# A two-layer mLSTM and retention trunk: when the heads' attention begins, and how layer 1's norm is transposed

## The chip, the cores and the metric

The kernel runs on one core of one Trainium2 chip. A core has five engines, each with a queue of its own: TensorE (PE in the profile, with PEld for its weight loads), VectorE (DVE), ScalarE (ACT), GpSimd (POOL) and SyncE (SP), which here issues the DMAs. SBUF is the memory on chip, PSUM the memory that PE writes its products to, DRAM lies outside. The metric is the time on the device in microseconds (us); lower is better.

## The reference

The input x has 1024 rows of 1024 columns. There are two layers, each with four mLSTM heads and four retention heads, 256 columns to a head:

```
for l in range(2):
    shift, scale, gate = split(silu(c) @ w_ada[l] + b_ada[l], 3)
    h = rmsnorm(x, norm_g[l]) * (1 + scale) + shift
    mq, mk, mv, mo, mz, mi, mf, rq, rk, rv, rz = split_cols(h @ w_in[l])
    mq, mk = silu(causal_conv4([mq, mk]))                 # along the rows, 4 taps
    y_m = sigmoid(mo) * layernorm(mlstm(mq, mk, mv, mi, mf)) * silu(mz)
    y_r = layernorm(retention(rotary(rq), rotary(rk), rv)) * silu(rz)
    x = x + gate * (concat(y_m, y_r) @ w_out[l])
return rmsnorm(x, final_g)
```

For mlstm and retention, row t of a head's output is a sum over the rows s up to t of (q_t . k_s) v_s with a weight that decays with t - s: in retention by a constant of the head, in mLSTM by gates computed from mi and mf, with a running maximum and a division at the end. All is float32.

## The kernel before

A float32 product is made of three matmuls on operands split in a high and a low part (`mm3`: lines 145, 146, 147); a split is a rounded copy on ACT (line 614) and a subtraction (line 615) on POOL or DVE. The projections' products go to PSUM tiles `pp`, four of them, those of attention and the transposes to `pa`, also four. The 1024 rows are two halves of 512 rows, and four chunks of 256 rows (`j` = 0 to 3). `hT[k][half]` is the normed input, transposed, for block k of 128 columns.

**Order.** PE's order is the order of the program text (`manual_schedule` for PE); the order of the other queues is set by a scheduler from the dependencies and its own estimates. The main loop runs units of projection work; after each comes a `tick`, which lets every launched generator take one step (`yield n` waits n ticks). A unit is 12 matmuls of 512 columns, or 24 of 256 in the values' projection `v_path`, which has eight units; after every second one a chunk's values are split (`v_split`, lines 600, 601, 604: two ACT copies, two DVE subtractions and, for mLSTM, two small casts). `launch(gen, d)` starts a generator d ticks later.

**A head.** Each head (`hg` = 0 to 7; 0 to 3 mLSTM, 4 to 7 retention) runs its gate projections (`gate_path`), its q and k projections (`qk_ml`, `qk_ret`), its values' projection and the generator `attention`. The steps of `attention` are: for mLSTM the load and the making of the decay masks `dm` of chunks 0 and 1 (`dm_load`, `dm_make`: lines 748, 750, 756, 757), then `scores(0)` and `scores(1)`, then for each chunk `values(j)`, `update` (the running state, split into `cH`, `cL`), `scores(j + 2)` and `finish(j)`. `scores` multiplies q by k on PE (line 765 in its diagonal form), multiplies the product by the mask on DVE (779, 780, 782, 789, 790), splits the result into `sH` (ACT) and `sL` (POOL) and loads the mask of chunk j + 2 into the buffer of its own (two buffers). `values(j)` multiplies `sH`, `sL` by the split values. The rows of k that `update` needs come back from DRAM (`k_rows`, lines 665, 666).

For heads 1 and 2 attention is launched 7 ticks, for head 3 4 ticks behind the start of `v_path`. For heads 4 to 7 it is launched when both projections are done; head 4 runs `v_path` ahead of q and k, the others behind. Between `scores(1)` and `values(0)` there is one tick, for head 0 two. Behind head 1 of layer 0 the rotary tables are made (`rotary_tables`, lines 374 to 390) in steps of their own. Retention's rotary tables are loaded again at the end of head 3 (`load_rotary`).

**The output projection** runs in two halves of the rows, each with two column halves (`out_units`, lines 952 to 956 for its loads of `g` and `ndr`). When layer 0's rows of a half are done, `norm_later` scales them and, in eight steps, transposes four blocks on PE (line 315), scales and shifts the result from PSUM (lines 321, 323) and splits it to layer 1's `hT[k][half]`. For half 0 this runs beside the output projection of half 1.

## Time and profile before

| | us |
|---|---|
| median of 3 runs | 2312.35 (2310.91 to 2312.63) |
| the profiled execution, its own time | 2311.88 |
| its span, first to last instruction | 2310.0 |

| engine | busy us | share of the span |
|---|---|---|
| PE | 2277.8 | 99% |
| DVE | 1353.2 | 59% |
| ACT | 907.1 | 39% |
| POOL | 823.5 | 36% |

How the rows are read. A timeline row has start, duration, engine, line, operation, output<-inputs and shape; matmuls are pipelined, so a row of PE lasts longer than the distance to the next one's start, and it is that distance that adds up. A row of the waits has the engine and line that waited, what it waited for, and the total, the number and the longest in us. A row of the groups has the shape, xcount, busy us and mean ns, and behind the last bar the engine's idle time ahead of it with what ended it. A row of the windows has the stretch, its length, busy us (x instructions) of PE, PEld, DVE, ACT and POOL, the granted TensorE clock (1.00 is full), the DMA engines' busy share and GB/s.

### The profile page before, as it was taken

What the parts mean: (1) busy time and instruction counts of PE and PEld (TensorE: products, weight loads), DVE (VectorE), ACT (ScalarE), POOL (GpSimd) and SP (SyncE); (2) the same over time, 40 slices, a digit from 0 to 9 for tenths busy, and PEclk for the clock granted to TensorE, in tenths of its full rate; (3) what the DMA queues carried; (4) which work ended last, traced back from release to release, by engine and by line L of the source; (5) the groups of instructions that cost most, each with busy time, mean ns of one, the idle gap of its engine ahead of it and who ended that gap; (6) DMA issues with size and microseconds to landing.
All of it is one profiled execution on the core that took longest, in us unless ns stands there. A gap on an engine that the chain in (4) does not pass through costs nothing.

```text
span 2310.0 us, 34281 instructions
## 1 busy us (share of the span) xinstructions
PE 2277.8 (99%) x12447; PEld 1958.2 (85%) x12447; DVE 1353.2 (59%) x2835; ACT 907.1 (39%) x1768; POOL 823.5 (36%) x817
## 2 busy tenths in 40 slices
PE   7999999999999999999999999999999999999998
PEld 5888888889988888888888889888898888988886
DVE  7477688556555555584536665555563545556753
ACT  5535433444332323353434544344443323224442
POOL 1343424333343334222552434233334334341323
PEclk9999999999999999999999999999999999999999
DMA  8223232324433533486532322322323333436762
GB/s 257 80 64 98 73 84 80 82 74 116 120 109 88 150 83 87 128 258 217 177 92 57 84 72 77 84 74 69 81 70 89 81 87 93 124 81 205 240 231 78
DMA packets 328761, 259.44 MB, mean 112 GB/s; under 512 B 79732, under 2 KB 263804, under 8 KB 328592
## 3 DMA queue, kind: packets, MB, share of 16 engines
q1 hardware_dynamic: 328592, 257.27, 38.6%
q8 instruction: 97, 1.59, 0.3%
q14 instruction: 72, 0.59, 0.1%
HBM read 201.58 MB, written 55.61 MB: 111 GB/s over the span
## 4 chain that ended last, share of the span: by engine, by line
PE 91%; DVE 3%; DMA 3%; issue 1%; POOL 1%; ACT 1%; SPq 0%; POOLq 0%; DVEq 0%; ACTq 0%
PE pp L145 24%; PE pp L146 24%; PE pp L147 24%; PE pa L146 5%; PE pa L147 5%; PE pa L145 5%; PE pa L765 2%; DMA b<-in_w_ada_dram 1%; DMA b<-in_x_dram 1%; PE pa L315 0%; DMA raw<-in_w_ada_dram 0%; POOL wL L615 0%; POOL sL L615 0%; DVE b L266 0%; DMA b<-in_w_in_dram 0%
## 5 line engine op out<-in xcount | busy, mean ns | idle before, releaser
L145 PE MATMUL pp<-b,wH 128*128 128x512 f32 x1776 | 703.7, 396 | 1.1 <-ACT b L1137 1.1
L146 PE MATMUL pp<-b,wH 128*128 128x512 f32 x1776 | 700.2, 394 | 0.3 <-DVE b L1140 0.2
L147 PE MATMUL pp<-b,wL 128*128 128x512 f32 x1776 | 700.2, 394 | 0.0
L615 POOL TENSOR_TENSOR wL<-raw,wH 128x512 fp32r<-128x512 f32 x338 | 450.1, 1338 | 507.4 <-ACT wH L614 466.8
L147 PEld LDWEIGHTS pp<-b,wL 128*128 128x128 f32 x1776 | 333.9, 188 | 79.0
L146 PEld LDWEIGHTS pp<-b,wH 128*128 128x128 f32 x1776 | 334.2, 188 | 72.2 <-DVE b L1140 2.0
L145 PEld LDWEIGHTS pp<-b,wH 128*128 128x128 f32 x1776 | 334.4, 188 | 71.5 <-ACT b L1137 1.6
L614 ACT CAST wH<-raw 128x512 fp32r<-128x512 f32 x402 | 246.1, 616 | 322.8 <-PE pp L147 93.8
L145 PE MATMUL pp<-wH,b 128*128 128x256 f32 (+1 forms) x1152 | 353.0, 306 | 0.7 <-DVE g L543 0.7
L147 PE MATMUL pp<-wH,b 128*128 128x256 f32 (+1 forms) x1152 | 352.8, 306 | 0.0
L146 PE MATMUL pp<-wL,b 128*128 128x256 f32 (+1 forms) x1152 | 352.2, 306 | 0.0
L615 POOL TENSOR_TENSOR b<-acc,b 128x256 fp32r<-128x256 f32 (+1 forms) x208 | 200.8, 984 | 322.8 <-ACT b L614 315.2
L145 PEld LDWEIGHTS pp<-wH,b 128*128 128x128 f32 x1152 | 216.9, 188 | 12.3 <-DVE g L543 1.6
L147 PEld LDWEIGHTS pp<-wH,b 128*128 128x128 f32 x1152 | 216.6, 188 | 11.4
L146 PEld LDWEIGHTS pp<-wL,b 128*128 128x128 f32 x1152 | 216.7, 188 | 10.8
L632 DVE SCALAR_TENSOR_TENSOR acc<-pp,cols,acc 128x511 f32<-128x511 f32 (+2 forms) x192 | 142.5, 742 | 43.2 <-ACT acc L627 41.2
L614 ACT CAST b<-acc 128x256 fp32r<-128x256 f32 (+1 forms) x208 | 93.7, 487 | 187.4 <-DVE acc L709 127.6
L615 POOL TENSOR_TENSOR sL<-th,sH 128x384 fp32r<-128x384 f32 (+1 forms) x64 | 61.0, 953 | 236.5 <-ACT sH L614 171.9
L145 PE MATMUL pa<-wH,b 128*128 128x512 f32 x256 | 101.1, 395 | 0.0
L147 PE MATMUL pa<-wH,b 128*128 128x512 f32 x256 | 101.0, 394 | 0.0
L146 PE MATMUL pa<-wL,b 128*128 128x512 f32 x256 | 100.9, 394 | 0.0
L636 ACT ACTIVATE th<-acc 128x512 f32<-128x512 f32 x64 | 40.5, 632 | 146.3 <-DVE acc L634 79.3
(255 smaller groups left out, 3439.3 us busy)
## 6 DMA issues: line engine op xcount, KB each, us to landing
raw<-in_w_in_dram SPq DMA_DIRECT2D x274, 256.0 KB
raw<-in_w_out_dram SPq DMA_DIRECT2D x128, 256.0 KB
gdr<-g SPq DMA_DIRECT2D x64, 256.0 KB
ndr<-zt SPq DMA_DIRECT2D x128, 128.0 KB
raw<-in_w_ada_dram SPq DMA_DIRECT2D x64, 256.0 KB
g<-gdr SPq DMA_DIRECT2D x64, 256.0 KB
acc<-ndr SPq DMA_DIRECT2D x64, 256.0 KB
acc<-kdr SPq DMA_DIRECT2D x192, 64.0 KB
```

Source lines behind the costliest of these rows:

```text
L145: PE.matmul(o, lt[0], rt[0], start=start, stop=False)
L146: PE.matmul(o, lt[0], rt[1], start=False, stop=False)
L147: PE.matmul(o, lt[1], rt[0], start=False, stop=stop)
L614: A.copy(dst[0], src)
L615: eng.tensor_tensor(dst[1], src, f(dst[0]), ALU.subtract)
L632: V.scalar_tensor_tensor(acc[:, d:], pt[:, 0:HALF - d], wcol, acc[:, d:], ALU.mult, ALU.add)
L636: A.activation(th, acc, AF.Tanh, scale=0.5)
L765: PE.matmul(pd, kk[i][:, o:o + P], qd, start=dt == 0 and i == 0, stop=dt == 1 and i == 1)
```

## The change

Heads 1 to 7 launch `attention` with no delay ahead of `v_path`, so that its first step is taken at the first tick of the values' projection. Between `scores(1)` and `values(0)` there is still one tick for heads 1 to 3; for the retention heads there are now two. Head 4 runs q and k first and its values' projection behind, as the others do, and head 5's first gate projection takes the place that head 4's values' projection had. In `norm_later` the first half isn't transposed by PE: DVE transposes blocks of 32 x 32 (`V.transpose`), four DMAs for each quarter of the columns store them to DRAM (`hdr`) so that the blocks fall in place, two loads bring the transposed tiles back into the buffers of `dm`, and DVE scales and shifts them from SBUF. The second half stays as it was.

```diff
--- before.py
+++ after.py
@@ -912,7 +912,7 @@
         scores(0)
         yield 1
         scores(1)
-        yield 2 if hg == 0 else 1
+        yield 1 if 0 < hg < 4 else 2
         for j in range(NCH):
             whole = j in WHOLE
             values(j, (0, 1) if whole else (0,))
@@ -1013,12 +1013,42 @@
         G.tensor_tensor(rs[:, 0:n], s, mhalf[:, 0:n], ALU.pow)
         return [rs[:, tt:tt + 1] for tt in range(n)]
 
+    hdr = [dpool.tile([8, 32, HALF], F32, name=f"hdr{s}") for s in range(4)]
+
     def norm_later(l, xt, ss, hT, half):
         sst = row_rstd(ss, "nrm")
         norm_scale(xt, sst)
-        yield 4
-        for k in range(KT):
-            norm_split(l, norm_transpose(xt, k), hT, half, k)
+        if half:
+            yield 4
+            for k in range(KT):
+                norm_split(l, norm_transpose(xt, k), hT, half, k)
+                yield 1
+            return
+        yield 1
+        for s in range(4):
+            z = wt("zt", 1024, 1)
+            z4 = z.rearrange("p (b t c) -> p t b c", b=8, c=32)
+            for tt in range(4):
+                V.transpose(z4[:, tt:tt + 1], xt[tt][s // 2][:, (s % 2) * CH:(s % 2 + 1) * CH]
+                            .rearrange("p (a b c) -> p a b c", a=1, c=32))
+            for tb in range(4):
+                Q.dma_start(hdr[s][:, :, tb * P:(tb + 1) * P].rearrange("b j t -> j b t"),
+                            z[tb * 32:(tb + 1) * 32, :].rearrange("p (b t) -> p b t", b=8))
+            yield 2
+            hrs = []
+            for m in range(2):
+                hr = wt("dm", 512, 2)
+                Q.dma_start(hr, hdr[s].rearrange("b j t -> (b j) t")[m * P:(m + 1) * P])
+                hrs.append(hr)
+            yield 2
+            for m, hr in enumerate(hrs):
+                k = 2 * s + m
+                hf = wt("acc", 512, 4)
+                V.tensor_scalar(hf.rearrange("p (a b c) -> p a b c", a=4, c=32),
+                                hr.rearrange("p (b a c) -> p a b c", a=4, c=32),
+                                gsh[l][:, 0, k:k + 1], gsh[l][:, 1, k:k + 1], ALU.mult, ALU.add)
+                hT[k][half] = (bt(F32R), bt(F32R))
+                split_to(hT[k][half], hf)
             yield 1
 
     def final_scale(xn, rs, tt, half, fg):
@@ -1211,26 +1241,25 @@
                 rot = [[], []]
             if hg > 0:
                 gp = gp1 if hg == 1 else [[None, None], [None, None]]
-                run_units(gate_path(l, hg, hT, gp, 0, 1 if hg == 7 else 2, hg > 1 or l > 0))
+                run_units(gate_path(l, hg, hT, gp, 0, 1 if hg == 7 else 2, hg > 1 and hg != 5 or hg == 1 and l > 0))
             vs = []
             kt = [None] * NCH
             kT = [[None, None], [None, None]]
             qT = [[None] * NCH, [None] * NCH]
             if hg == 4:
-                run_units(v_path(l, hg, hT, gt, vs))
+                run_units(proj_units(load_w(w_in[l], zcol(5, 0), P), hT, z_evac([[None, None]], 0, gdr[l][5])))
             for which, res in ((0, qT), (1, kT)):
                 if ml:
                     run_units(qk_ml(l, hg, which, hT, gt, kt, res))
                 else:
                     run_units(qk_ret(l, hg % 4, which, hT, kt, res, *rot))
-            if 0 < hg < 4:
-                launch(attention(l, hg, gt, qT, kT, kt, vs, gp, rot), 4 if hg == 3 else 7)
-            if hg not in (0, 4):
+            attend = attention(l, hg, gt, qT, kT, kt, vs, gp, rot)
+            if hg > 0:
+                launch(attend, 0)
                 run_units(v_path(l, hg, hT, gt, vs))
-            if hg == 0:
+            else:
                 launch(v0_splits(gt, vraw, vs), 1)
-            if hg == 0 or hg > 3:
-                launch(attention(l, hg, gt, qT, kT, kt, vs, gp, rot), 2 if hg == 0 else 0)
+                launch(attend, 2)
             if hg == 7:
                 loads = OutLoads(l)
                 for _ in gate_path(l, hg, hT, gp, 1):
```

## The prediction

> **What bounds the kernel now.** I read the head of the page first, then the waits of TensorE (PE), then the timeline of single heads.

> ```profile
> span 2310.0 us, 34281 instructions
> ...
> PE 2277.8 (99%) x12447; PEld 1958.2 (85%) x12447; DVE 1353.2 (59%) x2835; ACT 907.1 (39%) x1768; POOL 823.5 (36%) x817
> ...
> PE 91%; DVE 3%; DMA 3%; issue 1%; POOL 1%; ACT 1%; SPq 0%; POOLq 0%; DVEq 0%; ACTq 0%
> ...
> PE pa L251 <- DVE b L246: 9.7, 2, 8.9
> ...
> PE pa L146 <- DVE cL L615: 1.7, 4, 0.5
> PE pa L147 <- POOL sL L615: 1.5, 2, 0.9
> PE pp L145 <- ACT b L1137: 1.1, 1, 1.1
> PE pa L145 <- DVE th L780: 1.0, 1, 1.0
> PE pa L145 <- ACT nd L839: 0.7, 1, 0.7
> ```

> PE is busy for 2277.8 of 2310.0 us and carries 91% of the chain. Behind the start (the 8.9 us at L251) it waits a dozen times, never longer than 1.1 us. So the time is PE's work plus its few waits, and the change can act in two ways: it takes PE instructions away, or it makes or removes waits. PE's own order is written in the program, so a wait isn't filled with other work: each microsecond of it is a microsecond of the end. DVE, ACT and POOL are under 60% busy, so only the order of their queues at one place can hurt. The sum starts from the profiled execution, 2311.88 us (its span plus 1.9 us); the median of the three runs is 2312.35, 0.47 above.

> **Attention beside its values' projection, heads 1 to 3.** A head's attention is a list of steps, one for each tick, where a tick is twelve matmuls of 512 columns or, in the values' projection, 24 of 256. Before, heads 1 to 3 took their first steps behind most of that projection (7 or, for head 3, 4 ticks late), so that at `scores(1)` the values had long been split. The step that follows, `values(0)`, came one tick behind `scores(1)`. Head 2 of layer 0:

> ```profile
> 424.66 0.63 PE L765 MATMUL pa<-b,b 128*128 128x256 f32 x4
> 425.13 0.40 PE L145 MATMUL pp<-b,wH 128*128 128x512 f32 x1
> ...
> 427.92 0.28 PE L145 MATMUL pa<-b,sH 128*128 128x258 f32 x1
> ...
> 428.16 0.28 PE L147 MATMUL pa<-b,sL 128*128 128x258 f32 x1
> ...
> 425.99 0.68 DVE L789 TENSOR_TENSOR th<-pa,dm 128x512 f32<-128x512 f32 x1
> ...
> 426.10 0.51 ACT L614 CAST sH<-th 128x384 fp32r<-128x384 f32 x1 [1.12 <-DVE th L782]
> 428.03 0.41 ACT L614 CAST sH<-th 128x256 fp32r<-128x256 f32 x1 [1.41 <-DVE th L790]
> ...
> 426.69 1.02 POOL L615 TENSOR_TENSOR sL<-th,sH 128x384 fp32r<-128x384 f32 x1 [5.20 <-ACT sH L614]
> 428.43 0.54 POOL L756 TENSOR_SCALAR_AFFINE_SELECT dm<-dm 128x128 f32<-128x128 f32 x2 [0.71 <-DMA dm<-mdr]
> ```

> The reader is to see how thin this is: `scores(1)` ends at 425.13, `sL` is ready at 427.71, and `values(0)`, which begins at 427.92, reads it in its third matmul at 428.16. Twelve matmuls in 425.13 to 427.92, 0.232 us apart, cover it with 0.45 us to spare.

> After the change, `scores(1)` stands at the 4th tick of the values' projection and `values(0)` at the 5th. The first values' block is finished at the 2nd, but its split into two parts (L600 on ACT, L601 on DVE, two tiles each) and the other decay masks are in the same queues. In the built program the queues behind `scores(1)` read, in order, at all six places (heads 1, 2, 3; two layers): DVE: L789, L666 twice, L782, L790, L666, L604, L666, L601, L604, L601. ACT: `sH` of chunk 0, `sH` of chunk 1, L665 twice, L600, L757 three times, L600. POOL: `sL` twice, L756 three times. The third L756 needs a mask whose buffer L789 has just freed, so its load is issued behind L789. The last L601 is needed by `values(0)`. Durations:

> ```profile
> L665 ACT ACTIVATE b<-acc,wd 128x256 fp32r<-128x256 f32 x48 | 21.8, 501 | 12.4 <-DMA acc<-kdr 12.4
> L600 ACT ACTIVATE b<-pp,eul 128x256 fp32r<-128x256 f32 x48 | 21.2, 469 | 13.2 <-DVE b L601 13.0
> ...
> L757 ACT ACTIVATE dm<-dm,COL 128x128 f32<-128x128 f32 x48 | 18.1, 399 | 14.9 <-POOL dm L756 14.8
> ...
> L757 ACT ACTIVATE dm<-dm,COL 128x256 f32<-128x256 f32 x16 | 8.1, 508 | 20.4 <-POOL dm L756 20.4
> ...
> L666 DVE SCALAR_TENSOR_TENSOR b<-acc,wd,b 128x256 fp32r<-128x256 f32 x48 | 29.7, 637 | 45.0 <-ACT b L665 45.0
> ...
> L601 DVE SCALAR_TENSOR_TENSOR b<-pp,eul,b 128x256 fp32r<-128x256 f32 x48 | 21.4, 474 | 1.9 <-ACT b L600 1.9
> ...
> L782 DVE TENSOR_TENSOR th<-th 128x128 f32<-128x128 f32 x32 | 12.4, 386 | 0.6
> ...
> L615 POOL TENSOR_TENSOR sL<-th,sH 128x256 fp32r<-128x256 f32 x32 | 27.3, 854 | 87.4 <-ACT sH L614 35.4 <-issue 34.8 <-PE pp L147 11.6
> ...
> L756 POOL TENSOR_SCALAR_AFFINE_SELECT dm<-dm 128x256 f32<-128x256 f32 x16 | 8.6, 540 | 29.2 <-DMA dm<-mdr 29.2
> ...
> 322.42 3.27 DMA dm<-mdr
> ...
> 400.06 0.28 PE L145 MATMUL pp<-wH,b 128*128 128x256 f32 x1
> ...
> 402.89 0.28 PE L145 MATMUL pp<-wH,b 128*128 128x256 f32 x1
> ```

> With 0 at the start of the tick that follows `scores(1)`: that tick lasts 402.89 − 400.06 = 2.83 us (24 matmuls), and the last L601 is needed some seven matmuls later, at 3.67. L789 runs 0.2 to 0.9 (0.68). Two L666 and L782 end at about 1.9 (back to back each takes some 0.1 to 0.2 less than its row: 0.4, 0.4, 0.3). `sH` of chunk 0 ends at 2.5 (0.51), `sL` at 3.55 (1.02), `sL` of chunk 1 at 4.3 (0.75 to 0.85). The mask's load is issued at about 0.95 and can be used 3.27 us later, at 4.2, or up to a microsecond after that if its issue waits in SP's queue. The three L756 end at about 5.2 to 5.4 (0.54 for two, then 0.4 to 0.54). On ACT, `sH` of chunk 1 ends at 2.9 (0.41), two L665 at 3.8, the first L600 at 4.2, and the L757 wait for POOL. The third ends at 5.9 (0.51), the second L600 behind it at 6.35 (0.47), the last L601 at 6.9 (0.47). So PE waits 6.9 − 3.67 = 3.2 us. Bounds: if nothing gets in another's way, 0.9 less (2.3); with the load a microsecond later, 4.3. The wait is in pieces: the first matmul needs the first L600 (4.2 against 2.83), the next ones L604 (4.8 or more), the later ones the last L601. I take 3.2 six times: **+19.2 us** (14 to 26). Nothing hides it: `values(0)` is next in PE's order.

> One row says how much the engines disturb each other there:

> ```profile
> 418.69 1.64 DVE L666 SCALAR_TENSOR_TENSOR b<-acc,wd,b 128x256 fp32r<-128x256 f32 x1 [5.72 <-ACT b L665]
> ...
> 417.51 3.98 POOL L615 TENSOR_TENSOR wL<-raw,wH 128x512 fp32r<-128x512 f32 x3
> ```

> L666 took 1.64 us against its mean of 0.64 while POOL split weights. In the chain above, two L666 fall beside the two `sL`; stretched like this they move the first L601 from about 4.7 to 5.2, still ahead of the third L757, which is why 3.2 stands and not more. [...]

> **The same for heads 4 to 7.** These have no masks to make, and `values(0)` now comes two ticks behind `scores(1)` (`yield 2`), so there are 5.7 us or more instead of 3.67 for the same splits without the three L757; they fit by 1 us. I estimate nothing, up to 0.5 us for each of the eight.

> **Head 4's order.** Its values' projection and one gate projection change places: the same PE instructions. The rotary tables' load now has one tick less ahead of its first use by DVE, but the projections' buffers let PE run on for several ticks: nothing, and up to the 1.1 us of the longest wait above if they didn't.

> **Layer 1's norm, first half.** Before, PE transposed eight groups of four blocks into the output projection:

> ```profile
> 1095.62 0.60 PE L315 MATMUL pa<-ident,b 128*128 128x128 f32 x4
> ...
> 1118.23 0.60 PE L315 MATMUL pa<-ident,b 128*128 128x128 f32 x4
> ```

> From the first to the last of the eight are 22.61 us, 3.23 for each tick; twelve matmuls 0.232 apart are 2.79. So a group costs 0.44 us and the eight **−3.55 us**. In their place come 16 DVE transposes, 16 stores and 8 loads (2 MB each way) and eight DVE scalings from SBUF instead of PSUM. They stand on DVE's and SP's queues in the output projection's second half of half 0. DVE has room behind them, and the transposed blocks are needed only when layer 1 begins. What can wait is DVE's own work for the output (L952, L956) behind a scaling that waits for its load, and the stores and loads in SP's queue ahead of weight loads: 0 to 2 us.

> **Waits that go or come.** The old waits of head 1 in layer 0 (L146 on `cL`, L145 on L780, L145 on `nd`: most of 1.7 + 1.0 + 0.7) lie beside the rotary tables, which now begin some eight ticks after attention's start instead of beside it. I take **−3** (−5 to 0). New small waits (head 5's splits behind BatchNorm statistics, the first output tiles, which lose some of head 7's attention as cover, the norm's loads): three places, each between nothing and 1.1 us, the longest wait now behind the start: **+2** (0 to 3.3).

> Sum: 19.2 − 3.55 − 3 + 2 = +14.65. 2311.88 + 14.65 = 2326.5, and 0.47 for the median: **2327.0 us**. With its bounds 14 − 3.55 − 5 + 0 = +5.5 and 26 − 3.55 + 3.3 = +25.7 (2318 to 2338).

> **Rivals.** *Faster: the second split isn't late.* If DVE and ACT get to the splits before the tick is over, because the mask is there early and POOL cuts it without delay, the six waits shrink and the gains stay. Gains are 3.55 + 3 = 6.55 us, so the point is 1.1 us a place; with none left it is 2312.35 − 6.55 = 2305.8. For it: head 2's `values(0)` holds today with 0.45 us to spare, and DVE has 41% idle time. Against it: the order in the queues is fixed, and even with the mask there at once, `sL` twice, the L756, the last L757, L600 and L601 follow `sH`: 2.5 + 1.02 + 0.75 + 0.9 + 0.5 + 0.45 + 0.45 = 6.6 against 3.67. Chance 0.11.

> *No change.* The places cost about 1.1 us each and balance the gains: 2312. Chance 0.07.

> *The output projection's start becomes bound.* Head 7's attention ends seven ticks earlier, so about 12 us of PE work leave the stretch in which DVE is fullest:

> ```profile
> 975.00:1035.00 60.00, 59.65 (x316) 50.66 (x315) 49.65 (x101) 31.51 (x55) 14.53 (x13) 1.00 0.77 247
> ```

> DVE is busy 49.65 of 60 us with DMA at 0.77. Against 48 us of PE, DVE would be 1.7 us short, less what of its work is attention's, or up to 3.5 us with the loads' delays; in two layers 3 to 7 more, on top of the forecast: 2333. For it: the share. Against: the steps that leave are DVE's work too. Chance 0.10.

> *The clock falls in the six waits.*

> ```profile
> 0.00:54.00 54.00, 37.36 (x159) 28.53 (x160) 39.72 (x84) 29.32 (x54) 7.63 (x13) 0.94 0.86 275
> 54.00:189.00 135.00, 134.84 (x706) 113.63 (x704) 81.58 (x160) 66.12 (x128) 51.41 (x55) 1.00 0.30 76
> ...
> 26.15 0.63 PE L145 MATMUL pp<-b,wH 128*128 128x512 f32 x1
> ...
> 29.57 0.63 PE L147 MATMUL pp<-b,wL 128*128 128x512 f32 x1
> ```

> Behind the start's long wait, matmuls began 0.43 us apart (eight from 26.15 to 29.57, 3.42 us instead of 1.86), at a granted clock of 0.94 over the window; later windows, with waits up to 1.1 us in the run, have 1.00. If a wait of 3.2 us has the same sequel, each costs 1.56 more: 6 × 1.56 = 9.4, so 2336. Against it: the wait comes in pieces with matmuls between. Chance 0.08. [...]

> **How the numbers follow.** The forecast keeps 0.64. Faster by over 0.2% (4.6 us, about what a measurement of this kernel can tell from no change) is most of the faster rival: 0.10. Within it are no change and the rest of that rival: 0.08. Slower: 0.64 + 0.10 + 0.08 = 0.82. The range runs from 2312, below which the faster rival is left out, to 2338, the forecast's own upper end and both slow rivals.

> **What would show it.** Right: in the waits of TensorE a new line of 12 rows or so, `pa` at L145 to L147 waiting for L600, L601 or L604, some 19 us in all, in six places just behind a 24-matmul tick; 32 transposes fewer at L315; ACT's third L757 ahead of the second L600, ended by POOL's L756, ended by the mask's load. The step is wrong if PE's waits there sum to under 7 us, or if the third L757 doesn't hold the second L600; the norm's step is wrong if the ticks at 1095 to 1119 don't shorten to 2.8 us; the forecast as a whole if the time is under 2312.

## The result, and the profile after

The changed kernel takes 2340.66 us (median, 2340.31 to 2342.27) against 2311.64 of the kernel before in the same runs: ratio 1.0127, 95% interval 1.0109 to 1.0144. It is slower by 29.0 us. The forecast was slower by 14.65, 2327.0 us, with a range that ended at 2338. The direction was right; the size and the range were not. The profiled execution is the slowest of the four, 2342.27 us, and its span is 30.5 us longer than the one before.

The head of the page after, then TensorE's waits (engine, line, what was waited for: us, times, longest):

```profile
span 2340.5 us, 34309 instructions
...
PE 2289.8 (98%) x12415; PEld 1965.8 (84%) x12415; DVE 1352.3 (58%) x2851; ACT 911.8 (39%) x1768; POOL 815.9 (35%) x817
...
PE pa L145 <- DVE b L604: 10.4, 6, 2.7
...
PE pa L146 <- DVE cL L615: 5.1, 7, 2.4
PE pa L146 <- DVE b L604: 3.6, 6, 0.7
...
PE pa L146 <- POOL wL L615: 0.9, 1, 0.9
PE pa L147 <- POOL b L615: 0.9, 1, 0.9
...
PE pa L146 <- DVE b L601: 0.4, 1, 0.4
```

The six places that the prediction named are there, six times each on L604. These rows (10.4 and 3.6) sum to 14.0 us and not to the 19 that was forecast for them; short gaps between the matmuls, which the list of waits leaves out, add to them, so below the loss is counted from the starts of the matmuls. And PE has 32 instructions fewer and is busy 12 us longer, which is no wait: its instructions themselves took longer. The timeline of head 1 in layer 0 shows where, first PE, then the chain on DVE, ACT and POOL that it waits for:

```profile
280.43 0.36 PE L145 MATMUL pa<-b,sH 128*128 128x258 f32 x1 [1.52 <-DVE b L604]
281.47 0.39 PE L146 MATMUL pa<-b,sH 128*128 128x258 f32 x1 [0.69 <-DVE b L604]
...
282.87 0.38 PE L146 MATMUL pa<-b,sH 128*128 128x258 f32 x1
...
283.51 0.42 PE L147 MATMUL pp<-wH,b 128*128 128x256 f32 x1
283.73 0.42 PE L145 MATMUL pp<-wH,b 128*128 128x256 f32 x1
...
286.86 0.28 PE L145 MATMUL pp<-wH,b 128*128 128x256 f32 x1
286.98 0.28 PE L146 MATMUL pp<-wL,b 128*128 128x256 f32 x1
```

```profile
276.08 0.69 DVE L789 TENSOR_TENSOR th<-pa,dm 128x512 f32<-128x512 f32 x1 [1.28 <-PE pa L765]
...
280.19 0.58 DVE L666 SCALAR_TENSOR_TENSOR b<-acc,wd,b 128x256 fp32r<-128x256 f32 x1
...
282.33 0.48 DVE L601 SCALAR_TENSOR_TENSOR b<-pp,eul,b 128x256 fp32r<-128x256 f32 x1 [0.92 <-ACT b L600]
...
280.53 1.40 ACT L757 ACTIVATE dm<-dm,COL 128x128 f32<-128x128 f32 x3 [0.74 <-POOL dm L756]
281.84 0.46 ACT L600 ACTIVATE b<-pp,eul 128x256 fp32r<-128x256 f32 x1
...
278.39 1.86 POOL L615 TENSOR_TENSOR sL<-th,sH 128x384 fp32r<-128x384 f32 x2 [2.66 <-ACT sH L614]
280.21 1.18 POOL L756 TENSOR_SCALAR_AFFINE_SELECT dm<-dm 128x128 f32<-128x128 f32 x3
```

```profile
277.00:280.00 3.00, 1.91 (x16) 1.70 (x15) 2.04 (x6) 1.99 (x5) 1.61 (x2) 1.00 0.49 86
280.00:284.00 4.00, 2.74 (x14) 2.17 (x15) 2.60 (x8) 2.61 (x7) 1.62 (x5) 0.92 0.37 80
284.00:288.00 4.00, 4.00 (x25) 4.00 (x25) 1.79 (x11) 1.10 (x2) 0.70 (x1) 0.66 0.00 0
288.00:292.00 4.00, 4.00 (x36) 4.00 (x36) 2.12 (x5) 2.91 (x7) 0.00 (x0) 1.00 0.00 0
```

The reader is to see two things. The chain in the middle fence is the predicted one: L789 starts at 276.08, the pair of `sL`, then L756, the three L757, the second L600, and the last L601, which ends at 282.8, 6.7 us behind L789's start (the prediction's times: 0.2 and 6.9). One link differs: at all six places the three L756 follow the pair of `sL` on POOL directly, so POOL's own queue set them and not the mask's load. And from 283.5 to 286.7, when PE waits for nothing any more, its 256-column matmuls start 0.21 us apart instead of 0.118, at a granted clock of 0.66 in the mean over 284 to 288 (the column behind POOL's busy time). At 286.9 they are back at 0.12.

The time lost at a place is the distance between two starts on PE less the matmuls between them at their usual 0.118 (256 columns) or 0.232 us (512). From the last matmul ahead of `values(0)` (278.63) to 286.86 are 8.23 us for 28 matmuls, usually 3.33, so 4.9 are lost. Counted like this over the whole trace:

| where | lost before | lost after |
|---|---|---|
| the six `values(0)` of heads 1 to 3 | 0 | 4.9, 5.6, 4.6, 4.7, 4.8, 4.8: 29.4 |
| head 1, layer 0, beside the rotary tables | 4.0 | 2.1 |
| head 2's update, layer 0 (407 us after) | 0 | 1.5 |
| retention heads of layer 0 (778, 925 us before; 767, 799 us after) | 1.4 | 3.3 |
| first output tiles of layer 0 and 1 | 0.6, 0.6 | 1.6, 1.8 |
| output projection beside the norm (1159 us) | 0 | 1.2 |

Without the 3.5 us of transposes, and with a `cL` wait of 0.8 in layer 1 that went and one of 0.6 at 585 us that came, this sums to 30.6 us, where the span grew by 30.5.

### The profile page after: what moved, and what is told of

The parts are those of the page before. It is cut to its first block, busy times and chain, and to the rows that moved or that the text cites. A ratio compares the mean times of both kernels' runs of the same rounds, so it can differ in the third digit from the quotient of the medians.

```text
span 2340.5 us, 34309 instructions
## 1 busy us (share of the span) xinstructions
PE 2289.8 (98%) x12415; PEld 1965.8 (84%) x12415; DVE 1352.3 (58%) x2851; ACT 911.8 (39%) x1768; POOL 815.9 (35%) x817
## 4 chain that ended last, share of the span: by engine, by line
PE 84%; DVE 6%; issue 3%; DMA 3%; POOL 2%; ACT 2%; SPq 1%; POOLq 0%; DVEq 0%; ACTq 0%
PE pp L145 22%; PE pp L147 22%; PE pp L146 22%; PE pa L146 5%; PE pa L147 5%; PE pa L145 5%; PE pa L765 2%; DMA b<-in_w_ada_dram 1%; DVE acc L632 1%; DMA b<-in_x_dram 1%; POOL wL L615 1%; POOL sL L615 0%; DVE b L666 0%; DVE acc L637 0%; DMA raw<-in_w_ada_dram 0%
## 5 line engine op out<-in xcount | busy, mean ns | idle before, releaser
L145 PE MATMUL pp<-b,wH 128*128 128x512 f32 x1776 | 704.0, 396 | 1.1 <-ACT b L1167 1.1
L147 PE MATMUL pp<-b,wL 128*128 128x512 f32 x1776 | 700.6, 394 | 0.0
L146 PE MATMUL pp<-b,wH 128*128 128x512 f32 x1776 | 700.2, 394 | 0.2 <-DVE b L1170 0.2
L615 POOL TENSOR_TENSOR wL<-raw,wH 128x512 fp32r<-128x512 f32 x338 | 448.8, 1334 | 564.8 <-ACT wH L614 530.5
L147 PEld LDWEIGHTS pp<-b,wL 128*128 128x128 f32 x1776 | 334.0, 188 | 79.4
L146 PEld LDWEIGHTS pp<-b,wH 128*128 128x128 f32 x1776 | 334.1, 188 | 74.6 <-DVE b L1170 1.6
L145 PEld LDWEIGHTS pp<-b,wH 128*128 128x128 f32 x1776 | 334.2, 188 | 73.8 <-ACT b L1167 1.6
L614 ACT CAST wH<-raw 128x512 fp32r<-128x512 f32 x402 | 246.7, 617 | 365.0 <-PE pp L146 164.3
L147 PE MATMUL pp<-wH,b 128*128 128x256 f32 (+1 forms) x1152 | 356.0, 309 | 0.0
L146 PE MATMUL pp<-wL,b 128*128 128x256 f32 (+1 forms) x1152 | 355.9, 309 | 0.0
L145 PE MATMUL pp<-wH,b 128*128 128x256 f32 (+1 forms) x1152 | 355.9, 309 | 0.0
L615 POOL TENSOR_TENSOR b<-acc,b 128x256 fp32r<-128x256 f32 (+1 forms) x208 | 201.1, 987 | 349.0 <-ACT b L614 349.0
L145 PEld LDWEIGHTS pp<-wH,b 128*128 128x128 f32 x1152 | 220.9, 192 | 11.6
L146 PEld LDWEIGHTS pp<-wL,b 128*128 128x128 f32 x1152 | 220.6, 191 | 11.8
L147 PEld LDWEIGHTS pp<-wH,b 128*128 128x128 f32 x1152 | 220.6, 191 | 11.4
L614 ACT CAST b<-acc 128x256 fp32r<-128x256 f32 (+1 forms) x208 | 93.5, 487 | 218.0 <-DVE acc L709 149.3
L632 DVE SCALAR_TENSOR_TENSOR acc<-pp,cols,acc 128x511 f32<-128x511 f32 (+2 forms) x192 | 142.5, 742 | 41.7 <-ACT acc L627 39.6
L615 POOL TENSOR_TENSOR sL<-th,sH 128x384 fp32r<-128x384 f32 (+1 forms) x64 | 58.1, 912 | 150.8 <-ACT sH L614 95.3
L146 PE MATMUL pa<-wL,b 128*128 128x512 f32 x256 | 100.9, 394 | 0.9 <-POOL wL L615 0.9
L145 PE MATMUL pa<-wH,b 128*128 128x512 f32 x256 | 101.1, 395 | 0.0
L147 PE MATMUL pa<-wH,b 128*128 128x512 f32 x256 | 100.9, 394 | 0.0
```

Of the source, the lines that this page charges most:

```text
L145: PE.matmul(o, lt[0], rt[0], start=start, stop=False)
L146: PE.matmul(o, lt[0], rt[1], start=False, stop=False)
L147: PE.matmul(o, lt[1], rt[0], start=False, stop=stop)
L614: A.copy(dst[0], src)
L615: eng.tensor_tensor(dst[1], src, f(dst[0]), ALU.subtract)
L632: V.scalar_tensor_tensor(acc[:, d:], pt[:, 0:HALF - d], wcol, acc[:, d:], ALU.mult, ALU.add)
```

## The experiments

Each stands against runs of the kernel before on the same chip. The intervals of five of them (26 and 13 matmuls ahead, the late masks, the old norm, heads 1 to 3 alone) overlap that of the kernel after, 1.0109 to 1.0144, so what these five show of the parts is read from the places in their traces.

**26 matmuls more, ahead of values(0).** In `attention`, behind the `yield` that follows `scores(1)`:

```diff
+        if 0 < hg < 4:
+            pf = ps_a()
+            for i in range(26):
+                PE.matmul(pf[:, 0:CH], qT[0][0][:, 0:P], qT[0][0][:, 0:CH], start=True, stop=True)
```

> The kernel after, with 26 added matmuls of 256 columns on PE (operands q of chunk 0, result never read) just ahead of values(0) of heads 1 to 3 in both layers: 26 x 0.118 = 3.07 us, about as long as the wait that stands there. Nothing else in any queue changes its order. Theory (a wait of 3.2 us and, behind it, a stretch at half the clock): PE is kept busy, the waits shrink to under 0.5 us, matmuls behind them start 0.118 us apart at once, and the time falls by the clock's part, 6 x 1.5 to 2.2, to about 2330 us, although 156 matmuls were added. Rival (the slow stretch is paid for by the chain in the other queues, not by the clock): the time stays at 2340 or rises to 2345.

Measured 2336.91 us (2334.38 to 2340.01), ratio to before 1.0107 [1.0093, 1.0121]; its profiled span is 2335.0, 5.5 below the one after. The same head in its timeline (the added matmuls in one row) and windows:

```profile
279.40 3.28 PE L919 MATMUL pa<-b 128*128 128x256 f32 x26
...
282.51 0.28 PE L145 MATMUL pa<-b,sH 128*128 128x258 f32 x1
...
280.00:284.00 4.00, 4.00 (x34) 3.86 (x33) 2.96 (x8) 2.65 (x9) 2.26 (x6) 1.00 0.36 81
284.00:288.00 4.00, 4.00 (x36) 4.00 (x35) 1.79 (x11) 1.22 (x3) 0.70 (x1) 1.00 0.00 0
```

The added work fills the wait, the clock stays at 1.00 and 36 matmuls pass in 284 to 288 where 25 did. At the six places 29.4 us lost become 18.4 us of added matmuls, 1.6 us lost at head 2 of layer 0 and under 0.5 at each of the others. The expected 2330 was not reached: two other places lost more here (4.1 for 2.6 us at head 5's `cL`, where the clock now fell; 2.8 for 1.2 in the output projection).

**The same 26 matmuls behind values(0).** 

> The control to the kernel with 26 added matmuls: the same 26 matmuls at each of the six places, but just behind values(0) instead of ahead of it. Theory: the waits of 3 us stay, the clock falls behind them as in the kernel after, and the added matmuls cost their full time, 6 x 3.07 = 18.4 us or more where they run in the slow stretch: 2359 us or a little above. Rival (the added matmuls help wherever they stand): about 2337, as with the 26 ahead.

Measured 2356.78 us, ratio 1.0197 [1.0183, 1.0211]. So the same work costs 20 us more at the other side of `values(0)`: it isn't the work that helps but that PE isn't idle. In its trace the six places lose 29.2 us beside the added work, as in the kernel after, and the clock fell at five of them.

**13 matmuls.** 

> As the kernel with 26 added matmuls, with 13 (1.53 us) at each of the six places, so that a wait of about 1.5 to 1.7 us is left. If the clock falls only when PE idles for most of some 3 us, it stays at 1.00 and the time is that of the kernel with 26, about 2330 us. If a wait of 1.5 us is enough, the time is that of the kernel after, 2340.

Measured 2335.33 us, ratio 1.0101 [1.0085, 1.0116]; head 1 of layer 0 by its windows, and the wait that is left:

```profile
281.00:285.00 4.00, 3.27 (x21) 2.49 (x20) 2.59 (x9) 2.57 (x7) 1.46 (x5) 1.00 0.34 75
285.00:289.00 4.00, 4.00 (x35) 4.00 (x35) 1.79 (x11) 1.62 (x4) 0.70 (x1) 1.00 0.00 0
...
PE pa L146 <- DVE b L604: 3.5, 6, 0.6
PE pa L145 <- DVE b L604: 1.3, 1, 1.3
```

Five places lose 1.76 to 1.80 us with the clock at 1.00. At the sixth (head 2, layer 0, the row with 1.3), where the rows of k are late as well, 4.5 us are lost and the clock fell. So 1.8 us of lost time did not bring the clock down at five places, and what is left at the sixth did. The time is that of 26, as expected of the clock, though not 2330.

**Two ticks between scores(1) and values(0).**

```diff
-        yield 1 if 0 < hg < 4 else 2
+        yield 2
```

> The kernel after with two ticks instead of one between scores(1) and values(0) for heads 1 to 3. Theory: the splits of the first values' block have 2.83 us more, the six waits shrink from 3.2 to 0.4 us or nothing, the clock stays at 1.00, and the six places' 29.8 us go down to 0 to 3: 2311 to 2314 us. Rival (the late splits only move the wait to the next step, update or values(1), behind the same queues): 2325 or more.

Measured 2321.14 us, ratio 1.0039 [1.0026, 1.0051], between the two expectations. The six places lose 0.9, 1.8 and four times 0.5: 4.7 for 29.4, and the clock stays at 1.00 at all six. But one tick later head 1 meets the rotary tables again:

```profile
PE pa L145 <- DVE th L780: 2.8, 1, 2.8
```

There 4.6 us are lost (308 to 315 us) instead of 2.1, part of them at a granted clock of 0.50 from 311.7 to 315.1, and head 3's `update`, the output projection and layer 1's first output tiles lose 0.6 to 0.9 more each. The six waits were the cause of the most; the rest moved on in part.

**Masks out of ACT's queue.** The masks of chunks 2 and 3 are loaded and made behind `values(0)`:

```diff
-            dm_load(j + 2)
+            if not 0 < hg < 4:
+                dm_load(j + 2)
...
+            if j == 0 and 0 < hg < 4:
+                dm_load(2, True)
+                dm_load(3, True)
```

with a copy from `nd` into the buffer ahead of each load. 

> The kernel after, with the masks of chunks 2 and 3 of heads 1 to 3 loaded and made only behind values(0) (two small ACT copies from values(0)'s result into the mask's buffer make the load wait), so that no L757 and no L756 stands ahead of the second L600. If the masks in ACT's queue are what the last L601 waits for, the last L601 comes 0.6 to 0.7 us earlier, the six waits fall from 3.0 to about 2.3 us, and the time by 4 us, and by up to 10 more where the clock then stays: 2326 to 2337 us. If POOL's two sL with the L666 beside them are the bound, the waits stay at 3.0 and the time at 2340.

Measured 2334.48 us, ratio 1.0096 [1.0081, 1.0112]. ACT's and DVE's ends of the chain at head 1:

```profile
279.97 0.45 ACT L600 ACTIVATE b<-pp,eul 128x256 fp32r<-128x256 f32 x1
281.73 0.47 ACT L600 ACTIVATE b<-pp,eul 128x256 fp32r<-128x256 f32 x1 [1.31 <-DVE b L601]
...
276.72 0.69 DVE L791 TENSOR_TENSOR th<-pa,dm 128x512 f32<-128x512 f32 x1 [1.27 <-PE pa L767]
...
282.24 0.49 DVE L601 SCALAR_TENSOR_TENSOR b<-pp,eul,b 128x256 fp32r<-128x256 f32 x1 [0.47 <-ACT b L600]
```

(L791 is L789, two lines down.) The last L601 starts 5.52 us behind it instead of 6.25, 0.73 earlier; the six places lose 24.6 us instead of 29.4. So ACT's queue was the end of the chain, as said. What is then last is the first L601 on DVE, behind the L666, and most of each wait stays: the clock fell at five of the six places, and the one without a fall (1432 us) still lost 2.7.

**The old norm, attention changed.** `norm_later` as before, all else as after. 

> The kernel after with the norm of layer 1 as before (PE transposes its first half too). Theory: the eight groups of transposes cost 8 x 0.44 = 3.55 us again, and the one wait of 1.1 us that stands in the output projection of the kernel after (at 1159 us) goes: 2340.7 + 3.55 - 1.2 = 2343.0 us. Rival (the trip through DRAM delays more than it saves): 2340.5 or less.

Measured 2341.12 us, ratio 1.0124 [1.011, 1.0138], between the two. It settles the norm badly, because the clock fell at four of the six places here instead of six, and at two of the four for 6.8 us instead of 3.4. It does show equal waits with and without a fall of the clock. Head 3 of layer 0, first in this kernel, then in the kernel after; the waits are the same, 1.52 or 1.53 and 0.58 us. The windows are cut on the steps of 3.413 us on which all changes of the clock in each trace lie (see the last section):

```profile
553.53 0.36 PE L145 MATMUL pa<-b,sH 128*128 128x258 f32 x1 [1.52 <-DVE b L604]
554.47 0.39 PE L146 MATMUL pa<-b,sH 128*128 128x258 f32 x1 [0.58 <-DVE b L604]
...
550.48:553.89 3.41, 1.89 (x14) 1.51 (x13) 2.45 (x7) 2.24 (x6) 2.40 (x4) 1.00 0.35 78
553.89:557.31 3.42, 2.69 (x18) 2.29 (x19) 2.02 (x8) 2.31 (x7) 0.79 (x3) 1.00 0.27 56
```

```profile
551.05 0.35 PE L145 MATMUL pa<-b,sH 128*128 128x258 f32 x1 [1.53 <-DVE b L604]
551.98 0.39 PE L146 MATMUL pa<-b,sH 128*128 128x258 f32 x1 [0.58 <-DVE b L604]
...
549.57:552.98 3.41, 1.34 (x7) 0.97 (x7) 2.39 (x6) 2.64 (x9) 2.62 (x6) 1.00 0.52 105
552.98:556.40 3.42, 3.39 (x15) 3.09 (x16) 2.20 (x11) 0.76 (x3) 0.22 (x1) 0.50 0.00 0
```

One loses 3.3 us, the other 4.6. The waits are the same, but in this kernel they are divided over two stretches, with 14 and 18 matmuls, and in the kernel after they lie in one, with 7, and the clock is at half in the next.

**The parts, each alone on the kernel before.** Heads 1 to 3 launched at the first tick:

> The kernel before with heads 1 to 3 alone launched at the first tick of their values' projection, with one tick between scores(1) and values(0); heads 4 to 7 and the norm as before. Theory: this alone makes the six waits with their slow stretches (29.8 us in the kernel after), head 2's wait for the rows of k (1.5), and takes 2.1 us of head 1's old waits: 2312.2 + 29.2 = 2341 us, or up to 6 us less where the clock doesn't fall at some of the six. Rival (much of it comes from heads 4 to 7): under 2332.

Measured 2337.68 us, ratio 1.0114 [1.01, 1.0127]; the clock fell at all six places, which lose 28.4 us. That is 26.4 us over the kernel before (2311.25), so heads 1 to 3 alone make most of the 29.0. Heads 5 to 7 alone (head 4's order kept, since the rotary tables' load hangs on head 3's end):

> The kernel before with heads 5 to 7 alone launched ahead of their values' projection, with two ticks between scores(1) and values(0). Theory: no wait at values(0); the waits for cL of head 5 (2.6 us for 0.8 before) and at the first output tiles (1.6 for 0.6; 1.8 for 1.4) come: +3 us, 2315 us. Rival (heads 4 to 7 are free, the waits belong to head 4's new order or to heads 1 to 3): 2312.2.

Measured 2313.00 us against 2311.25, ratio 1.0006 [0.9997, 1.0015]: the size leans to the first, the interval holds no change. Its trace has the waits: 2.2 us lost at head 5's `cL` (none there before; the 0.8 at 925 us, which the expectation gives to head 5, belongs to head 6 and is gone), 1.5 and 1.75 at the first output tiles (0.6 and 0.6 before). What head 5's wait hangs on is in the kernel after: the norm of one head's values (L884, L886) stands ahead of `cL` on DVE:

```profile
796.96 0.56 POOL rsd L884
797.54 1.21 DVE nmu L886
798.75 0.61 DVE cL L615
799.41 0.39 PE pa L146
```

The norm alone:

> The kernel before with the new norm of layer 1's first half alone. Theory: eight groups of transposes go, 8 x 0.44 = 3.55 us, and one wait of 1.1 to 1.2 us for split weights comes in the output projection (it stood at 1159 us in the kernel after): 2312.2 - 3.55 + 1.2 = 2309.8 us. Rival (stores and loads in SP's queue hold weight loads and DVE's work up by more than is saved): 2312 or more.

Measured 2309.38 us against 2311.25, ratio 0.9992 [0.9983, 1.0001]: as expected in size, though the interval just holds no change. The new wait is there, in the chain that ended last:

```profile
1135.70 0.32 SPq L1000
...
1136.07 0.46 SPq L1035
...
1136.62 3.14 DMA raw<-in_w_out_dram
...
1139.86 0.63 ACT wH L614
...
1140.56 1.29 POOL wL L615
...
1141.89 0.50 PE pa L146
```

The last store of the norm (L1035) stands in SP's queue behind the row stores (L1000), which wait for DVE, and the weights' load stands behind it. The three parts alone sum to 26.4 + 1.8 − 1.9 = 26.3 us; the other 2.7 no run takes apart, and head 4's new order was not run alone.

**Three tries at a better one.** The norm's quarters three ticks apart instead of five:

> The kernel before with the new norm alone, its four quarters three ticks apart instead of five, so that its last stores and loads leave SP's queue before the row sums and stores of the other half's first columns begin. Theory: the wait of 1.0 us at 1142 us (weights' load behind the last store and the x stores in SP's queue) goes: 2309.4 - 1.0 = 2308.4 us. Rival (loads of ndr held up by the denser stores make a wait of their own): 2309.4 or more.

Measured 2310.17 us against 2311.58, ratio 0.9995 [0.9986, 1.0004]. The wait at 1142 went and one of 2.0 us at 1108 took its place. With the rotary tables ten ticks later as well:

> The kernel with the early norm, and the rotary tables of head 1 in layer 0 begun ten ticks later. Theory: head 1's old waits beside the tables (0.9 + 1.2 + 0.8 + 0.9 us, 315 to 338 us in the kernel before) mostly go: 3 us less than the early norm alone, 2305.5 us. Rival (the tables' work meets head 2's attention instead): no less.

Measured 2313.90 us, ratio 1.0009 [1.0, 1.0017]: head 1's four old waits are gone, and one place in head 2's conv loses 7.0 us (408 to 418 us), because the tables' instructions (L387 to L400, `rotary_tables` goes on to there) fill DVE from 402.9 to 410.2, ahead of the L632 and L634 for which PE waits; that wait is 4.5 us, and the clock is at 0.50 from 410.9 to 417.7. Four ticks and five ticks:

> The kernel before with the new norm, its quarters four ticks apart, and the rotary tables begun five ticks later. If the norm's waits (1.0 to 2.0 us) and head 1's old waits (3.8 us) both go without others in their place: 2311.5 - 3.55 - 3 = 2305 us. If they only change places, as with three ticks and ten ticks: 2309 to 2313 us.

Measured 2315.78 us, ratio 1.0013 [1.0004, 1.0022], above both expectations: 3.8 us are lost at head 1, 4.6 at head 2 (with a fall of the clock) and 2.3 beside the norm at 1115. No version tried is shown to beat the kernel before; the norm alone comes nearest.

## Why the prediction was right or wrong

*The six waits: right, in place, size and chain, but for the mask's load.* 19.2 us were forecast. Without a fall of the clock such a place loses 3.3 us (head 3 in the kernel with the old norm); five of these and about 4.5 for head 2 in layer 0 (its first wait is 2.75 us where head 3's is 1.53) are 21.0, an estimate, since the clock fell at all six. What wasn't seen is head 2's extra microsecond, where L665 and L666 wait for rows of k that are late.

*The clock: the step that failed.* The prediction had it as a rival with a chance of 0.08 and a price of 9.4 us, and set it aside because "the wait comes in pieces with matmuls between". The pieces did not help: 29.4 − 21.0 = 8.4 us went into matmuls at 0.21 us. The reading that it rested on was wrong too: it took the slow matmuls at the start for the sequel of the 8.9 us wait, which had ended at 12.73. The trace of before, cut finer:

```profile
19.94:23.35 3.41, 1.53 (x8) 0.87 (x8) 2.99 (x3) 1.47 (x3) 3.41 (x3) 1.00 1.05 395
23.35:30.18 6.83, 5.77 (x13) 4.27 (x14) 6.34 (x16) 3.71 (x10) 1.38 (x2) 0.50 1.09 359
```

The waits in the first of these stretches are 0.42, 0.44 and 0.97 us. So the trace of before already had a fall behind a stretch in which PE idled in short pieces, and a stretch with PE idle most of the time should have been added up as one. The forecast with that rival's price, 2336.4, is 4.3 below what was measured.

*Small new waits: mis-sized.* Forecast +2 with an upper bound of 3.3; measured 6.6 (1.5 at head 2's update, 0.6 at head 3's, 1.9 at the retention heads of layer 0, 1.0 and 0.4 at the first output tiles net of others in layer 1, 1.2 beside the norm). The bound was the longest wait of the old trace, 1.1 us, and that is no bound for places where the work stands anew: head 5's `cL` alone took 2.6.

*Old waits that go:* −3 forecast, −1.9 measured. *The transposes:* −3.55 forecast; twelve matmuls there take 2.79 us in the kernel with the norm alone, as forecast, instead of 3.23, so −3.5. The span with the norm alone is only 1.2 us shorter because 2.2 us more are lost in waits, 1.0 at 1142 us and 1.2 at one of head 1's old waits. *Heads 4 to 7 at `values(0)`:* nothing was forecast, and 0.6 to 0.7 us at head 5 of layer 0 is all that came. *The start of the output projection* didn't become bound: 1.6 and 1.8 us there, not 3 to 7 on top.

Sum by measured terms: 21.0 + 8.4 + 6.6 − 1.9 − 3.5 = 30.6, of a span that grew by 30.5.

## What to carry to other kernels

When a step is moved nearer to what feeds it, count the instructions that stand ahead of its last input in each queue, not the engines' shares: the six waits of over 3 us came on engines that were under 60% busy. A wait on TensorE can cost more than its length: here 3.3 us lost in pieces brought 1.3 to 1.6 us more at a clock of 0.50, and 1.8 us brought none, so idle pieces that lie in one of the 3.41 us stretches seen in these traces are to be added up before they are priced. And the longest wait of a trace bounds only the places that were in it.

## What the runs showed of the hardware

In these runs the clock did not follow the length of a wait alone. Behind the same waits of 1.5 and 0.58 us (head 3 of layer 0) the clock stayed at 1.00 in the kernel with the old norm and fell to 0.50 in the kernel after; of the six places, which lost about 3.3 us or more to waiting, all fell in the kernel after and four in the one with the old norm; a single wait of 1.8 to 2.4 us at head 5's `cL` brought a fall in three kernels and none in five.
